# A decoder block in one launch: values copied into both halves of the array, and the embedding's projection moved to the attention

## The chip, the cores and the metric

The kernel runs on one core of a Trainium2 chip. The metric is the device time of one execution in microseconds (us). The engines of the core have a queue each and work through it in order: PE (TensorE: matrix products), DVE (VectorE) and ACT (ScalarE) for elementwise work, POOL (GpSimd, hardly used here) and SP (SyncE, which here only issues DMA transfers). ACT issues some transfers too, in its own order between its other work. Engines wait for each other by semaphores. On-chip memory is SBUF; products land in PSUM, from which DVE and ACT read.

## The reference, cut to what matters

One layer, 256 tokens, width 2048, all in float32. Attention and state-space branch are mixed by gates, then come a feed-forward network and an embedding that is added through a gate.

```python
def hybrid_layer(x, p_i, ...):
    h = rms_norm(x, norm_mix_w)
    q, k, v, z, xbc, dt_raw, gate_a, gate_s = jnp.split(h @ w_in, ...)
    attn = sliding_window_attention(rms(q), rms(k), v, attn_sinks, rel_bias_table) @ w_attn_out
    ssm = mamba2_mixer(z, xbc, dt_raw, ...) @ w_ssm_out
    x = x + (sigmoid(gate_a) * attn + sigmoid(gate_s) * ssm) @ w_out
    u = causal_depthwise_conv(rms_norm(x, norm_ffn_w) @ w_ffn_up, ...)
    g, up = jnp.split(u, 2, axis=-1)
    x = x + (gelu(g) * up) @ w_ffn_down
    ple_gate = sigmoid(rms_norm(x, ple_norm_w) @ w_ple_gate)
    return x + ple_gate * (p_i @ w_ple_proj)      # p_i: (256, 256), w_ple_proj: (256, 2048)
```

The attention has 32 heads of 64, four groups of keys and values (8 heads share one), a window of 128 tokens, a bias by distance and a sink per head. The bias is a table (32 distances' buckets by 32 heads); the kernel gets it by a product with a one-hot matrix.

## The kernel before, in words

**Products.** Every weight matrix is cut into panels of 256 output columns, a panel into chunks of four k-steps of 128 rows (512 KB, or 256 KB for the embedding's two k-steps). A chunk is loaded by SP into a buffer `raw` (five of them), ACT copies it rounded into `wh` (line 71), DVE computes the remainder `wl` (line 72); of `wh` and `wl` there are three each. Activations stand as two rounded parts side by side. A k-step is four products: `wh` against both parts (512 columns, line 87), twice, and `wl` against the first part (256 columns, line 89), twice. The two results of a panel are accumulated in two of the four PSUM banks `acc`; then ACT copies the second part out (`lo`, line 133) and DVE adds (`sum`, line 135). Other products use four more banks, `ms`.

**Stages.** State-space branch with its products (XS: the normalised input); gate panels; `w_ssm_out` over YS; then the attention: the K panel and the V panel (`by_token`, lines 553 to 555), and eight panels for queries in turn with eight gate panels by the list ATT_ORDER; then `w_attn_out` over AS, `w_out`, the feed-forward network, and the tail: eight panels of `w_ple_gate` over XG.

**Attention.** Heads go in 16 pairs. A pair is a Python generator (`attend`), and after each weight chunk `advance` moves up to three running pairs by one step: bias load (by ACT's queue); transpose of the queries (line 610) and their split Q (616, 617); scores (623, 624), bias (626, 627), maxima (629, 630); exponentials on ACT (640) and scaling on DVE (647); transposes of the probabilities (653) and their copies `pts` (654); products with V (662); and the split of the result into AS (140, 141). The products with V have 64 stationary columns: the first head of a pair writes to partitions 0 to 63 and the second to 64 to 127, in three steps of 128 columns. When the list of panels ends, the last pairs are moved to their end (the drain).

**Embedding.** In the tail a function `embedding` computes, one panel ahead of its use, the two k-steps of `p @ w_ple_proj` with the same helpers, into `ms` banks.

**What sets the order.** A scheduler puts every engine's instructions in an order of its own by its model of durations, with the program's order as a priority; then each engine's order is fixed. Buffers of a name share slots, and the memory of a pool that has been released is reused: the attention's small tiles, `tab` among them, take over YS's memory, so they wait for the last product that reads YS.

Of the kernel before, what the change touches and what calls it, by code (L numbers as in the profile page):

```python
# [10 lines left out]
F32 = mybir.dt.float32  # L11
F32R = mybir.dt.float32r
# [33 lines left out]
def hybrid_block(ctx: ExitStack, tc: tile.TileContext, a: dict, out: bass.AP):  # L46
# [10 lines left out]
    def acc():  # L57
        return acc_pool.tile([P, 512], F32, name="acc")

    def misc():  # L60
        return ms_pool.tile([P, 512], F32, name="ms")
# [76 lines left out]
    def split(dst, src):  # L138

        S.activation(dst[:, 0:T], src, AF.Copy)  # L140
        V.tensor_tensor(dst[:, T:2 * T], src, dst[:, 0:T].bitcast(F32), ALU.subtract)
# [347 lines left out]

    m_pool = tc.alloc_tile_pool(name="mp", bufs=1, side="right")  # L490
# [3 lines left out]
    with tc.tile_pool(name="att", bufs=2) as ap:  # L494
# [5 lines left out]
        oneh = ap.tile([N_BUCKETS + 1, RLEN], F32, name="oneh", bufs=1)  # L500
# [3 lines left out]
        rsb = ap.tile([N_HEADS, RLEN], F32, name="rsb", bufs=1)  # L504
# [4 lines left out]
        def pair_bias(i):  # L509
            t = ap.tile([P, 2, 2 * P], F32, name="bias", bufs=4)  # L510
            nc.scalar.dma_start(t, bass.AP(rdr.tensor, rdr.offset + 2 * i * RLEN, [[1, P], [RLEN, 2], [1, 2 * P]]))
            return t
# [80 lines left out]
        vt = ap.tile([P, 2, 256], F32, name="vt", bufs=1)  # L593
        psv = by_token()
        for b in range(2):
            vu = ap.tile([P, 256], F32, name="ksq")
            V.tensor_scalar(vu, psv[b][:, 0:PW], r_tok[:, b:b + 1], None, ALU.mult)
            pv = misc()
            TE.matmul(pv[:, 0:PW], lhsT=flip, rhs=vu, start=True, stop=True)
            S.activation(vt[:, b, :], pv[:, 0:PW], AF.Copy)  # L600

        def attend(i, qn):
# [52 lines left out]
            yield  # L655
            o = misc()
            vs = slice(g * HD, (g + 1) * HD)
            for cs, b, ks, f, e in ((slice(0, P), 0, slice(0, P), True, True),
                                    (slice(P, T), 0, slice(P, T), True, False),
                                    (slice(P, T), 1, slice(T, 384), False, True)):  # L660
                for h in range(2):
                    TE.matmul(o[h * HD:(h + 1) * HD, cs], lhsT=vt[:, b, vs], rhs=pts[:, h, ks], start=f, stop=e)  # L662
            split(AS[:, i, :], o[:, 0:T])
# [11 lines left out]
        for kind, pn in ATT_ORDER:  # L675
            if kind == "q":
                qn = normed(by_token(advance))
                waiting += [(2 * pn, qn), (2 * pn + 1, qn)]
                continue
            ps2 = panel(W, base, ND, XS, between=advance)  # L680
            base += CH
            for i in range(2):
                t = summed(ps2[i])
                V.tensor_tensor(GA[:, 2 * pn + i, :], t, r_bc, ALU.mult)
        while waiting or running:
            advance()
# [77 lines left out]
    with tc.tile_pool(name="ple", bufs=2) as pp:  # L764
        pt_ = pp.tile([P, 2, T], F32, name="pt_", bufs=1)
        nc.scalar.dma_start(pt_, a["pT"])
        PS_ = pp.tile([P, 2, 2 * T], F32R, name="PS_", bufs=1)
        for k in range(2):
            split(PS_[:, k, :], pt_[:, k, :])
        _, r3_bc = stat_to_rstd([sqb], "ple")  # L770
        def embedding(pn):
            wh, wl = load_chunk(a["w_ple_proj"][pn], 2, PW)
            ps2 = [misc(), misc()]
            for k in range(2):
                products(ps2, wh[:, k, :], wl[:, k, :], PS_[:, k, :], k == 0, k == 1)
            return [summed(ps, "ple", 4, pp) for ps in ps2]

        for pn in range(8):
            if pn:
                es = embedding(pn)  # L780
            ps2 = panel(a["w_ple_gate"], pn * CH, ND, XG, joined=(pn == 7))
            if not pn:
                es = embedding(pn)
# [114 lines left out]
```

## Time and profile before

| | |
|---|---|
| Median of three runs | 2064.15 us (2063.41 to 2065.93) |
| The profiled execution | 2064.66 us, its span 2062.9 us |
| PE busy | 2035.7 us, 99% |
| DVE, ACT busy | 1451.1 us (70%), 1171.5 us (57%) |
| Chain that ended last | PE 87%, ACT 2%, DVE 1% |

PE is busy nearly all the time, so the first thing to look for are the few stretches in which it isn't. The times of instructions on PE overlap: an instruction's length is longer than the distance to the next, and what a group of them costs is read from start to start. A fp32 product (not split into rounded parts) shows as two instructions.

### The profile page before, as it was taken

To read this page: it belongs to the slowest core of one execution; us is meant where nothing else is said; L and a number is where in the kernel's file an instruction comes from. 1 tells how busy PE (TensorE), PEld (TensorE's weight loads), DVE (VectorE), ACT (ScalarE), POOL (GpSimd) and SP (SyncE) were. 2 spreads that over 40 slices of the span, in tenths; PEclk is the share of its full clock that TensorE was granted. 3 is DMA by queue.
4 is the path that set the end of the run, shared out by engine and by line. 5 is a ranking of instruction groups with operands and counts; after the bars stand their busy time and mean duration, and the time that the engine had idled before them with its cause. 6 is when DMAs were issued, how large, how long until landed. Compare 5 with 4: busy or idle time off the path is not lost.

```text
span 2062.9 us, 32543 instructions
## 1 busy us (share of the span) xinstructions
PE 2035.7 (99%) x12448; PEld 1797.2 (87%) x12448; DVE 1451.1 (70%) x2502; ACT 1171.5 (57%) x1878; POOL 60.2 (3%) x54
## 2 busy tenths in 40 slices
PE   8999999999999999999989999999999999999999
PEld 7888888888888889998868888888888888888888
DVE  7888787778655546777766677777777776555576
ACT  6686677665544444656555556555555555444454
POOL 0000000000000000100000120000000000000000
PEclk9999999999999999999999999999999999999999
DMA  7556555545555556544435655555555555555564
GB/s 254 206 173 204 183 185 184 194 155 183 189 189 194 189 189 197 179 163 159 165 102 194 234 196 186 193 187 193 194 188 190 194 188 190 194 189 189 186 203 148
DMA packets 113736, 385.50 MB, mean 187 GB/s; under 512 B 13995, under 2 KB 21036, under 8 KB 112428
## 3 DMA queue, kind: packets, MB, share of 16 engines
q1 hardware_dynamic: 104492, 366.00, 51.8%
q10 hardware_dynamic: 9088, 17.43, 2.4%
q8 instruction: 97, 1.59, 0.3%
q14 instruction: 59, 0.48, 0.1%
HBM read 381.16 MB, written 2.21 MB: 186 GB/s over the span
## 4 chain that ended last, share of the span: by engine, by line
PE 87%; ACT 2%; DVE 1%; issue 0%; DVEq 0%
PE acc L87 51%; PE acc L89 26%; PE acc L554 2%; PE acc L553 2%; PE acc L555 2%; PE ms L662 1%; PE ms L653 1%; ACT E L238 1%; PE acc L95 1%; PE ms L451 0%; ACT wh L71 0%; PE ms L87 0%; PE ms L624 0%; PE ms L623 0%; DVE wl L72 0%; ACT L240 0%
## 5 line engine op out<-in xcount | busy, mean ns | idle before, releaser
L72 DVE TENSOR_TENSOR wl<-raw,wh 128x1024 fp32r<-128x1024 f32 (+1 forms) x704 | 846.6, 1205 | 536.3 <-ACT wh L71 533.1
L71 ACT ACTIVATE wh<-raw 128x1024 fp32r<-128x1024 f32 (+1 forms) x704 | 733.3, 1044 | 774.9 <-PE acc L87 459.6
L87 PE MATMUL acc<-XS,wh 128*128 128x512 f32 x1792 | 564.8, 397 | 9.4 <-ACT wh L71 9.4
L87 PE MATMUL acc<-XG,wh 128*128 128x512 f32 x1632 | 506.5, 392 | 0.0
L89 PEld LDWEIGHTS acc<-XS,wl 128*128 128x128 f32 x1792 | 335.1, 189 | 81.3 <-DVE wl L72 8.7
L89 PEld LDWEIGHTS acc<-XG,wl 128*128 128x128 f32 x1632 | 306.4, 188 | 67.4
L89 PE MATMUL acc<-XS,wl 128*128 128x256 f32 x1792 | 361.2, 282 | 3.7 <-DVE wl L72 3.6
L89 PE MATMUL acc<-XG,wl 128*128 128x256 f32 x1632 | 322.3, 279 | 0.0
L87 PEld LDWEIGHTS acc<-XS,wh 128*128 128x128 f32 x1792 | 275.6, 189 | 13.3 <-ACT wh L71 10.2
L87 PEld LDWEIGHTS acc<-XG,wh 128*128 128x128 f32 x1632 | 247.2, 188 | 0.0
L87 PE MATMUL acc<-FS,wh 128*128 128x512 f32 x704 | 218.4, 392 | 0.0
L87 PE MATMUL acc<-YS,wh 128*128 128x512 f32 x512 | 158.8, 392 | 0.0
L89 PEld LDWEIGHTS acc<-FS,wl 128*128 128x128 f32 x704 | 132.2, 188 | 29.0
L89 PE MATMUL acc<-FS,wl 128*128 128x256 f32 x704 | 138.9, 279 | 0.0
L89 PEld LDWEIGHTS acc<-YS,wl 128*128 128x128 f32 x512 | 96.1, 188 | 21.2
L87 PEld LDWEIGHTS acc<-FS,wh 128*128 128x128 f32 x704 | 106.6, 188 | 0.0
L89 PE MATMUL acc<-YS,wl 128*128 128x256 f32 x512 | 101.0, 279 | 0.0
L554 PE MATMUL acc<-wl,XS 128*128 128x256 f32 x320 | 90.9, 284 | 0.0
L555 PE MATMUL acc<-wh,XS 128*128 128x256 f32 x320 | 90.1, 282 | 0.0
L553 PE MATMUL acc<-wh,XS 128*128 128x256 f32 x320 | 90.1, 282 | 0.0
L87 PE MATMUL acc<-AS,wh 128*128 128x512 f32 x256 | 82.9, 401 | 2.9 <-DVE sum L135 1.8
L87 PE MATMUL acc<-MS,wh 128*128 128x512 f32 x256 | 79.4, 392 | 0.0
(233 smaller groups left out, 2106.7 us busy)
## 6 DMA issues: line engine op xcount, KB each, us to landing
raw<-in_w_in SPq DMA_DIRECT2D x256, 512.0 KB, 3.5
raw<-in_w_ffn_up SPq DMA_DIRECT2D x176, 512.0 KB, 3.2
raw<-in_w_ffn_down SPq DMA_DIRECT2D x88, 512.0 KB, 3.2
raw<-in_w_ssm_out SPq DMA_DIRECT2D x64, 512.0 KB, 3.2
raw<-in_w_attn_out SPq DMA_DIRECT2D x32, 512.0 KB, 4.2
raw<-in_w_out SPq DMA_DIRECT2D x32, 512.0 KB, 4.3
raw<-in_w_ple_gate SPq DMA_DIRECT2D x32, 512.0 KB, 3.2
acb<-acd ACTq DMA_DIRECT2D x8, 1024.0 KB, 4.6
```

The costliest lines, as they stand in the source:

```text
L71: S.activation(wh[:, ks, :], raw[:, ks, :], AF.Copy)
L72: V.tensor_tensor(wl[:, ks, :], raw[:, ks, :], wh[:, ks, :].bitcast(F32), ALU.subtract)
L87: TE.matmul(ps, lhsT=wh[:, cs], rhs=x, start=first, stop=False, skip_group_check=True)
L89: TE.matmul(ps[:, 0:T], lhsT=wl[:, cs], rhs=x[:, 0:T], start=False, stop=last, skip_group_check=True)
L95: TE.matmul(ps[:, 0:T], lhsT=w[:, cs], rhs=x[:, h * T:(h + 1) * T], start=first and n == 0, stop=last and n == 2)
L238: S.activation(E[:, h, :], acb[:, h, c, :], AF.Relu, scale=-1.0, bias=acs[:, c, hs.start + h:hs.start + h + 1])
L553: TE.matmul(ps2[b][:, 0:PW], lhsT=hi, rhs=wh[:, k, :], start=(kk == 0), stop=False)
L554: TE.matmul(ps2[b][:, 0:PW], lhsT=hi, rhs=wl[:, k, :], start=False, stop=False)
L555: TE.matmul(ps2[b][:, 0:PW], lhsT=lo, rhs=wh[:, k, :], start=False, stop=(kk == ND - 1))
L653: TE.transpose(pt[:, d * P:(d + 1) * P], Ls[:, h, c:c + P], ident)
L662: TE.matmul(o[h * HD:(h + 1) * HD, cs], lhsT=vt[:, b, vs], rhs=pts[:, h, ks], start=f, stop=e)
```

## The change

Four edits. The values `vt` are stored with each group's 64 columns twice, so that one product yields both heads in both halves of the partitions: two products a pair (512 and 256 columns) in place of six, and the split of the result by halves. The one-hot matrix and the row `rsb` take slots of the `raw` buffers, `bias` has three buffers in place of four. The embedding's eight panels stand behind the last gate panel, before the drain, with an `advance` after each; their accumulators are `acc` banks, and their sums go to a DRAM tile `emb` by SP's queue. The tail loads them from there by ACT's queue.

```diff
+    emb = dram.tile([ND, P, T], F32, name="emb")
...
-        oneh = ap.tile([N_BUCKETS + 1, RLEN], F32, name="oneh", bufs=1)
+        oneh = wp.tile([P, RLEN], F32, name="raw", bufs=5)[0:N_BUCKETS + 1, :]
         nc.sync.dma_start(oneh, a["onehot"])
...
-        rsb = ap.tile([N_HEADS, RLEN], F32, name="rsb", bufs=1)
+        rsb = wp.tile([P, RLEN], F32, name="raw", bufs=5)[0:N_HEADS, :]
...
-            t = ap.tile([P, 2, 2 * P], F32, name="bias", bufs=4)
+            t = ap.tile([P, 2, 2 * P], F32, name="bias", bufs=3)
...
-        vt = ap.tile([P, 2, 256], F32, name="vt", bufs=1)
+        vt = ap.tile([P, 2, N_KV, 2, HD], F32, name="vt", bufs=1)
...
-            S.activation(vt[:, b, :], pv[:, 0:PW], AF.Copy)
+            for h in range(2):
+                S.activation(vt[:, b, :, h, :], pv[:, 0:PW].rearrange("p (g d) -> p g d", g=N_KV), AF.Copy)
...
             o = misc()
-            vs = slice(g * HD, (g + 1) * HD)
-            for cs, b, ks, f, e in ((slice(0, P), 0, slice(0, P), True, True),
-                                    (slice(P, T), 0, slice(P, T), True, False),
-                                    (slice(P, T), 1, slice(T, 384), False, True)):
-                for h in range(2):
-                    TE.matmul(o[h * HD:(h + 1) * HD, cs], lhsT=vt[:, b, vs], rhs=pts[:, h, ks], start=f, stop=e)
-            split(AS[:, i, :], o[:, 0:T])
+            ov = o.rearrange("p (h t) -> p h t", h=2)
+            vd = vt.rearrange("p b g h d -> p b g (h d)")
+            TE.matmul(ov, lhsT=vd[:, 0, g, :], rhs=pts[:, :, 0:T], start=True, stop=False, skip_group_check=True)
+            TE.matmul(ov[:, :, P:T], lhsT=vd[:, 1, g, :], rhs=pts[:, :, T:384], start=False, stop=True,
+                      skip_group_check=True)
+            for h in range(2):
+                split(AS[half[h], i, :], ov[half[h], h, :])
...
+        pt_ = wp.tile([P, 2, T], F32, name="raw", bufs=5)
+        nc.sync.dma_start(pt_, a["pT"])
+        PS_ = ap.tile([P, 2, 2 * T], F32R, name="PS_", bufs=1)
+        for k in range(2):
+            split(PS_[:, k, :], pt_[:, k, :])
+        for pn in range(8):
+            wh, wl = load_chunk(a["w_ple_proj"][pn], 2, PW)
+            ps2 = [acc(), acc()]
+            for k in range(2):
+                products(ps2, wh[:, k, :], wl[:, k, :], PS_[:, k, :], k == 0, k == 1)
+            for i in range(2):
+                nc.sync.dma_start(emb[2 * pn + i], summed(ps2[i]))
+            advance()
         while waiting or running:
             advance()
...
-            if pn:
-                es = embedding(pn)
+            es = []
+            for i in range(2):
+                t = pp.tile([P, T], F32, name="ple", bufs=4)
+                nc.scalar.dma_start(t, emb[2 * pn + i])
+                es.append(t)
             ps2 = panel(a["w_ple_gate"], pn * CH, ND, XG, joined=(pn == 7))
-            if not pn:
-                es = embedding(pn)
```

The edits also move instructions that they don't name. First SP, from the last weights of `w_ssm_out` to the K panel's weights (`raw<-in_w_in`); before:

```order
29 L70 DMA raw<-in_w_ssm_out 128x1024 x64
30 L70 DMA raw<-in_w_in 128x1024 x7
31 L499 DMA tab<-in_rel_bias_table 32x32
32 L501 DMA oneh<-in_onehot 33x384
33 L515 DMA sink<-in_sinks 128x32
34 L519 DMA gq<-in_qk_gain 128x2
35 L564 DMA flip<-in_flip 128x128
36 L70 DMA raw<-in_w_in 128x1024 x65
```

and now:

```order
29 L70 DMA raw<-in_w_ssm_out 128x1024 x64
30 L502 DMA raw<-in_onehot 33x384
31 L500 DMA tab<-in_rel_bias_table 32x32
32 L516 DMA sink<-in_sinks 128x32
33 L520 DMA gq<-in_qk_gain 128x2
34 L565 DMA flip<-in_flip 128x128
35 L70 DMA raw<-in_w_in 128x1024 x72
```

Seven weight loads that stood ahead of `tab` stand behind it and the three small loads. On PE the product of `tab` and the one-hot matrix, which stood after 41 products of the K panel, is now the first behind YS.

Second, PE at the end of the drain (653 and 655: transposes of the probabilities; 662 and 663: products with V; AS: attention output), before:

```order
3592 L653 MATMUL ms<-c_ident,Ls 128x128 x6
3593 L662 MATMUL ms<-pts,vt 64x128 x6
3594 L653 MATMUL ms<-c_ident,Ls 128x128 x6
3595 L87 MATMUL acc<-AS,wh 128x512 x2
3596 L89 MATMUL acc<-AS,wl 128x256 x2
3597 L87 MATMUL acc<-AS,wh 128x512 x2
3598 L89 MATMUL acc<-AS,wl 128x256 x2
3599 L662 MATMUL ms<-pts,vt 64x128 x6
```

and now:

```order
3670 L655 MATMUL ms<-c_ident,Ls 128x128 x6
3671 L662 MATMUL ms<-pts,vt 128x512
3672 L663 MATMUL ms<-pts,vt 128x2x128
3673 L655 MATMUL ms<-c_ident,Ls 128x128 x6
3674 L662 MATMUL ms<-pts,vt 128x512
3675 L663 MATMUL ms<-pts,vt 128x2x128
3676 L87 MATMUL acc<-AS,wh 128x512 x2
3677 L89 MATMUL acc<-AS,wl 128x256 x2
```

Two k-steps of the attention output moved behind the last product with V. The embedding's products (PS_) stand earlier; their last ones, and the next transposes of a pair (it is pair 12, counted from 0), now:

```order
3562 L87 MATMUL acc<-PS__10959,wh 128x512
3563 L89 MATMUL acc<-PS__10959,wl 128x256
3564 L87 MATMUL acc<-AS,wh 128x512
3565 L89 MATMUL acc<-AS,wl 128x256
3566 L87 MATMUL acc<-AS,wh 128x512
3567 L89 MATMUL acc<-AS,wl 128x256
3568 L87 MATMUL acc<-AS,wh 128x512
3569 L89 MATMUL acc<-AS,wl 128x256
3570 L87 MATMUL acc<-AS,wh 128x512
3571 L89 MATMUL acc<-AS,wl 128x256
3572 L87 MATMUL acc<-AS,wh 128x512
3573 L655 MATMUL ms<-c_ident,Ls 128x128 x6
```

All 64 of them stand between the last product of the gates (row 3491) and this place.

## Rows read from the trace of the kernel before

**Rows 1.** the page: span; busy time and share of each engine.
```profile
span 2062.9 us, 32543 instructions
...
PE 2035.7 (99%) x12448; PEld 1797.2 (87%) x12448; DVE 1451.1 (70%) x2502; ACT 1171.5 (57%) x1878; POOL 60.2 (3%) x54
```

**Rows 2.** windows (length, busy times (instructions), granted clock, DMA share, GB/s).
```profile
1024.80:1045.80 21.00, 21.00 (x135) 18.36 (x133) 13.33 (x27) 16.45 (x34) 0.00 (x0) 1.00 0.50 164
1045.80:1071.30 25.50, 16.38 (x101) 12.60 (x99) 14.38 (x45) 13.18 (x40) 0.00 (x0) 0.87 0.09 31
...
1058.00:1065.00 7.00, 5.78 (x27) 4.75 (x28) 2.91 (x14) 4.19 (x14) 0.00 (x0) 0.52 0.00 1
```

**Rows 3.** PE timeline, drain (start, length, work; in brackets the wait).
```profile
1058.67 1.54 PE L653 MATMUL ms<-c_ident,Ls 128*128 128x128 f32 x6 [2.37 <-DVE Ls L647]
```

**Rows 4.** PE timeline of the tail, one embedding panel.
```profile
1995.41 0.62 PE L87 MATMUL ms<-PS__19888,wh 128*128 128x512 f32 x2
...
1996.79 0.39 PE L87 MATMUL acc<-XG,wh 128*128 128x512 f32 x1
```

**Rows 5.** PE timeline, products with V in one run.
```profile
1036.77 0.28 PE L89 MATMUL acc<-AS,wl 128*128 128x256 f32 x1
1036.98 0.88 PE L662 MATMUL ms<-pts,vt 128*64 128x128 f32 x12
...
1038.00 0.28 PE L624 MATMUL ms<-kl,Q 128*128 128x256 f32 x1
```

**Rows 6.** chain by time, products with V in two runs.
```profile
1018.33 0.36 PE ms L662 x2
...
1019.24 0.80 PE ms L662 x10
```

**Rows 7.** PE timeline, full fp32 products of 128 columns.
```profile
93.11 0.28 PE L89 MATMUL acc<-XS,wl 128*128 128x256 f32 x1
93.23 1.06 PE L443 MATMUL ms<-cbm,xde 128*128 128x128 f32 x8
...
94.25 0.63 PE L87 MATMUL acc<-XS,wh 128*128 128x512 f32 x2
```

**Rows 8.** SP timeline where the K panel begins.
```profile
775.23 5.85 SPq L70 DMA_DIRECT2D raw<-in_w_in  x3
781.44 0.34 SPq L499 DMA_DIRECT2D tab<-in_rel_bias_table  x1
...
783.15 0.43 SPq L564 DMA_DIRECT2D flip<-in_flip  x1
783.68 11.50 SPq L70 DMA_DIRECT2D raw<-in_w_in  x4
```

**Rows 9.** DMA issues (KB each, median us to landing).
```profile
raw<-in_w_in SPq DMA_DIRECT2D x256, 512.0 KB, 3.5
...
gno<-in_ssm_norm SPq DMA_DIRECT2D x1, 16.0 KB, 1.7
tab<-in_rel_bias_table SPq DMA_DIRECT2D x1, 4.0 KB, 4.0
```

**Rows 10.** PE and clock after an idle stretch early in the kernel.
```profile
215.35 1.22 PE L87 MATMUL acc<-XS,wh 128*128 128x512 f32 x2 [2.99 <-ACT wh L71]
...
215.30:222.00 6.70, 6.61 (x19) 5.12 (x20) 5.14 (x8) 4.44 (x7) 0.00 (x0) 0.50 0.68 234
```

**Rows 11.** ACT groups by shape (count, busy us, mean ns).
```profile
L133 ACT ACTIVATE lo<-acc 128x256 f32<-128x256 f32 x142 | 45.7, 372 | 2.5 <-PE acc L89 2.4
...
L640 ACT ACTIVATE Ls<-Ls,nm 128x256 f32<-128x256 f32 x32 | 16.0, 501 | 2.8 <-DVE nm L632 2.8
...
L71 ACT ACTIVATE wh<-raw 128x512 fp32r<-128x512 f32 x24 | 14.4, 622 | 8.1 <-issue 6.2 <-DMA raw<-in_w_in 0.9 <-PE acc L87 0.9
...
L694 ACT ACTIVATE GA<-GA 128x2048 f32<-128x2048 f32 x2 | 3.8, 1917 | 0.0
...
L694 ACT ACT_TABLE_LOAD x2 | 2.6, 1283 | 0.0
```

More of the change, by code (lines that the diff above doesn't have):

```diff
@@ L764, in hybrid_block @@
     with tc.tile_pool(name="ple", bufs=2) as pp:
[L765 to L769, printed above, removed]
-        _, r3_bc = stat_to_rstd([sqb], "ple")
[L771 to L776, printed above, removed]
-        for pn in range(8):
-            if pn:
-                es = embedding(pn)
+        _, r3_bc = stat_to_rstd([sqb], "ple")
+        for pn in range(8):
+            es = []
[3 more added lines that the diff above has]
+                es.append(t)
             ps2 = panel(a["w_ple_gate"], pn * CH, ND, XG, joined=(pn == 7))
-            if not pn:
-                es = embedding(pn)
             for i in range(2):
```

## The prediction

> **What bounds the kernel now.** I read the page's busy times first: PE is busy 2035.7 of 2062.9 us [rows 1], so an edit pays only where it takes products off PE or closes one of PE's few gaps, and it costs wherever it opens a new one. Next came the windows around the attention. Up to 1045.8 PE is full; from 1045.8 to 1071.3 it works 16.38 of 25.5 us, so 9.1 us are empty, and from 1058 to 1065 the granted clock is 0.52 [rows 2]. This is the drain: the last pairs of heads are softmax chains through DVE and ACT, and PE waits for them, up to 2.37 us at once [rows 3]. Then the timeline of the tail, for what the embedding's products cost where they stand. Then the timeline of the place where the K panel begins (781 us), because the order of SP changes there. The profiled execution took 2064.66 us, 0.5 over the median of the runs; the sum is made against it.
>
> **The embedding's products leave the tail.** A panel of them lies there between 1995.41 and 1996.79, among products that leave PE no gap [rows 4]: 1.38 us, eight panels, 11.0 us taken off a full PE. This gain is sure, and what the change does is decided by what the same 11.0 us cost in the new place. If they all filled empty time, the whole 9.1 us of the drain and some of its half clock would be won.
>
> **Where they stand now.** By the order of the changed program all 64 embedding products stand on PE before the transposes of pair 12, directly behind the last gate panel. There, between 1024.8 and 1045.8, PE was full before [rows 2]. The drain itself (the last two pairs: transposes, products with V, transposes, products with V) has no embedding product in it, and the two k-steps of the attention output that stood between its last two steps now stand behind them. So the embedding pushes later work back by its own length and the drain keeps its waits. Net of leaving the tail: 11.0 - 11.0 = 0.
>
> **What it meets there.** A chunk of the embedding is 1.38 us for PE; ACT has for it one conversion of 0.622 and two evacuations of 0.372 [rows 11], 1.37 us. So ACT has as much to do for it as PE, and has other work queued between. From the first embedding conversion to the evacuation of chunk 6's first half, ACT's order holds 8 conversions (5.0), 15 evacuations (5.6), one full weight conversion (at twice 0.622, 1.2), the sigmoid of the gates (1.92), two table loads (2.6), eight exponentials (at 0.501, 4.0) and eight copies for pairs 10 to 12 (at 0.372, 3.0): 23.3 us. The three weight buffers let ACT begin at most eight k-steps of 0.69 us (half a panel of the embedding [rows 4]) and some 2.5 us of attention products, 8.0 us, ahead of PE; I allow 3 us in which ACT itself waits for PE. It is done 23.3 - 8.0 + 3 = 18.3 us after PE begins the embedding, DVE's sum as much later as an evacuation takes. PE needs that accumulator (there are four) for the first product of the attention output after 11.0 us of embedding, 1.3 of V products, 1.0 of scores and perhaps 1.5 of smaller waits: 14.8. The wait is 3.9 us, with the smaller ones 5.4. Bounds: 0 if ACT's own waits vanish and it begins early, 9 if pair 12's exponentials come late too. I take 5.4. In the drain I credit 1.5 us: the two k-steps behind the last V products cover the waits for the last pair's result and for an accumulator. Against that each pair's output is now copied by halves, two ACT and two DVE instructions in place of one each, which lengthens its chain by about 0.4. Between -4 and +2, I take -1.5.
>
> **The K panel's first weights.** The one-hot matrix now takes a slot of the weight buffers, and with that the scheduler has drawn SP's order differently. Before, seven weight loads stood ahead of the load of the bias table, tab; now tab, sink, gains and flip stand ahead of all of them. tab's memory is freed by the last product with YS: its load was issued at 781.44, when those products ended, with the K panel's first loads already on their way since 775.23 [rows 8]. SP is in order, so all K panel loads now wait for the end of the YS products, and PE has nothing else: its next instruction is the small product with tab, then the K panel. The steps: tab at 781.44, three small loads, the first weight load some 0.45 earlier than the 783.68 of before (one load fewer between), 783.2; landing 3.5 later [rows 9], 786.7. On ACT the store of rdr stands ahead of the conversion and waits for the small product, so for tab: issue 781.44 plus 1.7 (the fastest small load) to 4.0 [rows 9], plus product, copy and issue, some 2 us, gives 785.1 to 787.4, about the same. Conversion of hi (at twice 0.622, 1.2) and of the remainder (as long): PE runs fully from 789.1. It lost 789.1 - 781.2 = 7.9, less some 0.9 of the small product that is now inside the stall (two instructions of 384 columns at 0.114 per 128 columns [rows 7], and 0.2 of entry): 7.0. Between 5.5 and 8.5 by the two ends of the landings. The nearest row for the clock is 215.35: after 2.99 us without work the granted clock is 0.50 through 6.7 us [rows 10], in which full work loses 3.3. So between 0 (it falls and is back before the work is) and 3.4 more; I take 2.5, nearer to the row. Nothing later gives this back, since PE is the bound. Together 9.5. bias with three buffers in place of four is no cost: its reloads stand behind the reads they wait for.
>
> **V in both halves.** Before, six products of 64 columns a pair; two halves run at once, and run and changes of mode hold PE from 1036.77 to 1038.00 [rows 5], 1.23 less the two normal steps of 0.115 around it, 1.0 us. Ten of the sixteen pairs are split in two runs by the order, and a split one holds PE for 0.36 + 0.80 [rows 6] and pays entry and exit, 0.2, twice: 1.56. 6 x 1.0 + 10 x 1.56 = 21.6 us. Now two full products over 512 and 256 columns. A full fp32 product of 128 columns takes two instructions, and eight of them hold PE from 93.11 to 94.25 less two steps of 0.115, 0.91, so 0.114 each [rows 7]; 768 columns are 12 of these, 1.37, or less, since fewer instructions carry it. At 1.33, 16 x 1.33 = 21.3, so -0.3. Between -1 and +4 (if entering fp32 costs 0.2 again).
>
> The Trainium skill (TensorEngine Tiling (Array Packing), Theoretical Speedup) speaks against this edit: with 64 stationary columns two tiles work at once, up to twice as fast, and the full form gives that up. The same page (Key Properties) says that a change of mode drains TensorE, and the trace agrees: 1.0 us held for some 0.65 of products. By the first rule alone the kernel would come to about 2088 (the fourth rival); with the drains counted, V is even.
>
> **Sum.** 0 (embedding) + 5.4 (waits beside it) - 1.5 (drain) + 9.5 (K panel) - 0.3 (V) = +13.1. From 2064.66 that is 2077.8; beside the median, 2077.
>
> **Rivals.** First, the drain is filled: ACT and DVE bring pairs 13 to 15 forward under the embedding, so that little is left to wait for. It wins up to 9.1, and with the half clock of 1058 to 1065 (5.78 busy, half of it lost, 2.9) [rows 2] 12.0; with the K panel's 9.5 and V's -0.3, -2.8, and -5 with the K panel at its lower end: 2062 to 2060. For it: the order was drawn to run other work beside the pairs. Against it: the last two pairs stand as bare as before. It decides from the point where the drain loses more than 9 us; 0.09. Second, it is filled by half and the embedding meets no waits: 9.5 - 0.3 - 7 = +2, 2066, no change; 0.09. Third, a load queue: SP now holds 16 stores of the embedding between the loads of the attention output, each waiting for a sum; if ACT's delay reaches them, one or two weight loads come late by a landing of 3.5 us: 2077.8 + 5 = 2083; 0.15. For it: SP is in order; against it: five weight slots ahead. Fourth, the changes of mode were hidden and the old form cost only its six pairs of instructions, 6 x 0.114 = 0.68 a pair: then V loses 16 x 0.65 = 10.4, 2088; against it stands the 1.0 us held [rows 5]; 0.04. The forecast has 0.63.
>
> **How the numbers follow.** A measurement can tell 0.2%, 4.1 us. Slower: forecast 0.63, third 0.15, fourth 0.04, and a third of the second 0.03: 0.85. Same: the rest of the second and a quarter of the first: 0.08. Faster: 0.07. The likeliest case alone spans 2070 to 2084 (K panel 5.5 to 11.9, embedding 0 to 9, not all at one end). The range reaches to the second rival: 2065 to 2085, which leaves out most of the first and the fourth.
>
> **What would show it.** Right: a wait of PE of some 7 us at 781, ended by the hi conversion, with half clock behind it; SP's first K load behind tab; PE gaps between the last gate panel and pair 12's transposes, released by sums and evacuations; the drain's bare steps as before; a tail shorter by 11 us. Wrong: PE full at 781, or a drain with less than 4 us empty.

## The result and the profile after

The changed kernel takes 2078.93 us (median of four runs, 2077.99 to 2080.30) against 2064.54 of the kernel before in the same comparison: ratio 1.0068, 95% interval 1.0056 to 1.0080. It is slower. The profiled execution took 2078.69 us, its span is 14.0 us longer than that of before.

The page of the changed kernel, span and busy times, answers to [rows 1]:

```profile
span 2076.9 us, 32419 instructions
...
PE 2037.7 (98%) x12320; PEld 1796.9 (87%) x12320; DVE 1460.1 (70%) x2518; ACT 1179.1 (57%) x1896; POOL 61.8 (3%) x54
```

PE's busy time grew by 2.0 us only, so twelve of the fourteen are empty time. To find it I cut the span at three products on PE that every kernel here has: the last that reads YS (w_ssm_out ends), the last that reads AS (attention output ends) and the last that reads FS (feed-forward ends). In us:

| | to YS's end | YS's end to AS's last | AS's last to FS's last | FS's last to the end |
|---|---|---|---|---|
| before | 781.09 | 358.04 | 817.92 | 105.82 |
| after | 780.54 | 384.11 | 817.93 | 94.32 |

The third column repeats to 0.01 us. So the stretches can be compared one by one, and the attention's stretch, with 11.0 us of embedding in it, is 26.1 us longer while the tail is 11.5 shorter. The waits of PE in it come in three places. First the K panel; the queue of SP there, from the changed kernel's timeline, answers to [rows 8]:

```profile
780.89 0.32 SPq L500 DMA_DIRECT2D tab<-in_rel_bias_table  x1
781.26 0.41 SPq L516 DMA_DIRECT2D sink<-in_sinks  x1
781.73 0.42 SPq L520 DMA_DIRECT2D gq<-in_qk_gain  x1
782.20 0.43 SPq L565 DMA_DIRECT2D flip<-in_flip  x1
782.72 1.80 SPq L70 DMA_DIRECT2D raw<-in_w_in  x4
```

On ACT, the store of rdr and the conversion behind it (start, length; in brackets the wait):

```profile
785.29 0.33 ACTq L508 DMA_DIRECT2D rdr<-raw  x1
786.37 1.06 ACT L71 ACTIVATE wh<-raw 128x1024 fp32r<-128x1024 f32 x1 [4.98 <-DMA raw<-in_w_in]
```

And PE's waits from there to the end of the drain, from its timeline (the embedding's products are those that read PS_; the drain answers to [rows 3]):

```profile
782.45 0.90 PE L504 MATMUL ms<-raw,tab 33*32 33x384 f32 x2 [1.64 <-DVE T L486]
787.48 0.80 PE L554 MATMUL acc<-wh,XS 128*128 128x256 f32 x2 [4.13 <-ACT wh L71]
788.74 0.58 PE L555 MATMUL acc<-wl,XS 128*128 128x256 f32 x1 [0.46 <-DVE wl L72]
...
1045.87 0.79 PE L87 MATMUL acc<-PS__10959,wh 128*128 128x512 f32 x1 [2.08 <-DVE sum L135]
...
1074.95 0.39 PE L625 MATMUL ms<-kh,Q 128*128 128x256 f32 x1 [1.15 <-DVE Q L619]
...
1083.94 1.54 PE L655 MATMUL ms<-c_ident,Ls 128*128 128x128 f32 x6 [2.50 <-DVE Ls L649]
1086.21 2.08 PE L662 MATMUL ms<-pts,vt 128*128 128x512 f32 x2 [0.73 <-ACT pts L656]
...
1091.34 1.12 PE L662 MATMUL ms<-pts,vt 128*128 128x512 f32 x2 [0.95 <-ACT pts L656]
...
1094.69 0.74 PE L87 MATMUL acc<-AS,wh 128*128 128x512 f32 x2 [0.39 <-DVE AS L141]
...
1098.30 0.51 PE L87 MATMUL acc<-AS,wh 128*128 128x512 f32 x1 [1.92 <-DVE sum L135]
```

The windows of the three places (length, busy times of PE, PEld, DVE, ACT, POOL, granted clock, DMA share, GB/s) answer to [rows 2]:

```profile
780.54:790.54 10.00, 3.77 (x15) 2.51 (x14) 4.65 (x10) 2.77 (x4) 0.00 (x0) 0.62 0.65 221
790.54:800.00 9.46, 9.46 (x74) 9.46 (x73) 3.67 (x3) 4.07 (x4) 0.00 (x0) 0.86 0.79 264
1028.94:1049.61 20.67, 16.54 (x79) 12.87 (x78) 16.57 (x43) 18.30 (x42) 0.00 (x0) 0.92 0.72 231
1049.61:1098.30 48.69, 38.66 (x201) 30.66 (x199) 29.10 (x70) 24.84 (x62) 0.00 (x0) 0.89 0.33 108
```

The K panel's stall is 6.2 us of empty PE, and the granted clock stays low well after it. Beside the embedding 4.1 us are empty, and ACT is busy for 18.30 of 20.67 us. From there to the end of the drain 10.0 are empty, where before it was 9.1. The waits for `pts` right ahead of the products with V are new or longer.

### The profile page after: what moved, and what is told of

It reads as the page before. It is cut to its first block, busy times and chain, and to the rows that moved or that the text cites. A ratio compares the mean times of both kernels' runs of the same rounds, so it can differ in the third digit from the quotient of the medians.

```text
span 2076.9 us, 32419 instructions
## 1 busy us (share of the span) xinstructions
PE 2037.7 (98%) x12320; PEld 1796.9 (87%) x12320; DVE 1460.1 (70%) x2518; ACT 1179.1 (57%) x1896; POOL 61.8 (3%) x54
## 4 chain that ended last, share of the span: by engine, by line
PE 86%; ACT 2%; DVE 1%; DMA 0%; issue 0%; SPq 0%; DVEq 0%; ACTq 0%
PE acc L87 50%; PE acc L89 26%; PE acc L555 2%; PE acc L556 2%; PE acc L554 2%; PE ms L662 1%; ACT E L238 1%; ACT wh L71 1%; PE acc L95 1%; PE ms L451 0%; PE ms L655 0%; DVE wl L72 0%; PE ms L663 0%; PE ms L626 0%; PE ms L625 0%
```

## The experiments

Each kernel ran beside the kernel before on its chip. For them the table gives the same stretches as above, the empty time of PE between the gates' last product and the last AS product, the median, and the ratio to the kernel before with its interval. FS's last to the end is 105.82 or 105.83 where the embedding stands in the tail, 94.31 to 94.33 where it stands in the attention (fill_early: 94.52).

| | to YS's end | YS's end to AS's last | empty | AS's last to FS's last | median | ratio |
|---|---|---|---|---|---|---|
| before | 781.09 | 358.04 | 9.1 | 817.92 | | |
| after | 780.54 | 384.11 | 14.2 | 817.93 | 2078.93 | 1.0068 (1.0056 to 1.0080) |
| raw_only | 783.51 | 367.76 | 9.0 | 817.93 | 2074.62 | 1.0046 (1.0032 to 1.0060) |
| small_early | 781.24 | 381.70 | 13.9 | 817.92 | 2076.95 | 1.0055 (1.0042 to 1.0067) |
| v_old | 784.28 | 381.68 | 12.7 | 817.92 | 2079.32 | 1.0067 (1.0054 to 1.0079) |
| no_embedding_move | 781.62 | 367.27 | 12.4 | 817.92 | 2074.43 | 1.0046 (1.0034 to 1.0059) |
| bias_before_YS | 789.50 | 374.40 | 14.5 | 817.93 | 2077.92 | 1.0065 (1.0052 to 1.0077) |
| V_alone | 786.11 | 360.76 | 11.7 | 817.93 | 2073.42 | 1.0045 (1.0031 to 1.0059) |
| fill | 790.14 | 371.77 | 12.7 | 817.92 | 2075.93 | 1.0046 (1.0033 to 1.0059) |
| fill_v_old | 791.13 | 367.34 | 8.4 | 817.92 | 2071.02 | 1.0032 (1.0019 to 1.0045) |
| bias_at_start | 787.57 | 377.75 | 15.6 | 819.64 | 2081.05 | 1.0075 (1.0062 to 1.0087) |
| six_sums | 780.82 | 384.93 | 14.3 | 817.93 | 2080.15 | 1.0070 (1.0057 to 1.0084) |
| fill_best | 788.65 | 364.35 | 7.1 | 819.59 | 2069.60 | 1.0021 (1.0013 to 1.0030) |
| fill_early | 779.27 | 365.59 | 6.9 | 819.80 | 2060.87 | 0.9981 (0.9972 to 0.9990) |

The first column needs care: before, after, raw_only, v_old and six_sums run the same work up to YS's end, and it ends between 780.54 and 784.28. A comparison of whole executions carries some of that spread of 3.7 us; a stretch from YS's end on does not. One source of the spread stands in the last section.

**raw_only**, one part of the change alone:

```diff
-        oneh = ap.tile([N_BUCKETS + 1, RLEN], F32, name="oneh", bufs=1)
+        oneh = wp.tile([P, RLEN], F32, name="raw", bufs=5)[0:N_BUCKETS + 1, :]
...
-        rsb = ap.tile([N_HEADS, RLEN], F32, name="rsb", bufs=1)
+        rsb = wp.tile([P, RLEN], F32, name="raw", bufs=5)[0:N_HEADS, :]
```

> The kernel before with one edit of the change alone: the one-hot matrix and rsb take slots of the weight buffers (V, bias and the embedding as before). SP's order has tab, sink, gains and flip ahead of all K panel loads, as in the changed kernel. Theory (the load of tab waits for the last YS product and holds the K panel's weights behind it): PE waits 6 us at 781, with half clock behind it for some 3 us of loss, and the kernel takes 2064.5 + 9 = 2073.5 us (2071 to 2076). Rival (the stall of the changed kernel has another source, its V or its embedding): no wait at 781, 2064.5 us (2063 to 2066).

Measured 2074.62, and the attention's stretch is 9.72 us longer than before. PE's long wait at the K panel:

```profile
790.60 0.80 PE L553 MATMUL acc<-wh,XS 128*128 128x256 f32 x2 [4.36 <-ACT wh L71]
```

The stall is the changed kernel's, with neither its V nor its embedding. What this doesn't tell is whether the order of SP or the two lent slots make it.

**small_early**, from the changed kernel: the four small loads out of YS's memory.

```diff
+        small = ev.tile([P, T], F32, name="rsq", bufs=2)
-        tab = ap.tile([N_BUCKETS + 1, N_HEADS], F32, name="tab", bufs=1)
+        tab = small[0:N_BUCKETS + 1, 0:N_HEADS]
...
-        sink = ap.tile([P, N_HEADS], F32, name="sink", bufs=1)
+        sink = small[:, N_HEADS:2 * N_HEADS]
...
-        flip = ap.tile([P, P], F32, name="flip", bufs=1)
+        flip = small[:, P:T]
```

> The changed kernel with tab, sink, gains and flip in one tile of the buffer rsq, whose memory is not YS's; SP issues the four loads early in the kernel, so that nothing that waits for YS stands ahead of the K panel's weights. The one-hot matrix and rsb still take two of the five weight slots. Theory (SP's order is the cause): PE is full at 781 (under 1 us empty, granted clock 1.00), 9 us less than the changed kernel, 2070 us (2068 to 2072). Rival (the two slots taken from the weight buffers are the cause, the order is not): the first K loads still come after 778, PE waits 4 us or more at 781 to 792, and the kernel stays at 2075 to 2079 us.

Measured 2076.95: the theory's number fails, and so does the rival's mechanism, because the K panel's loads now start at 769.86. SP, then ACT, then PE:

```profile
764.34 0.36 SPq L503 DMA_DIRECT2D raw<-in_onehot  x1
769.86 29.76 SPq L70 DMA_DIRECT2D raw<-in_w_in  x11
```

```profile
783.09 0.33 ACTq L509 DMA_DIRECT2D rdr<-raw  x1
783.52 2.95 ACT L71 ACTIVATE wh<-raw 128x1024 fp32r<-128x1024 f32 x3 [1.43 <-DVE T L486]
```

```profile
784.63 0.50 PE L555 MATMUL acc<-wh,XS 128*128 128x256 f32 x2 [2.35 <-ACT wh L71]
785.89 0.58 PE L556 MATMUL acc<-wl,XS 128*128 128x256 f32 x1 [0.76 <-DVE wl L72]
```

The weights are there, and ACT, in order, first waits for the copy of the small product (behind DVE's T) to store rdr. Half of the empty time goes (6.2 to 3.1 us), and the clock falls all the same: 0.50 from 786 to 790, 0.76 from 790 to 794. A second queue had stood behind the first.

**v_old**, from the changed kernel:

```diff
-            TE.matmul(ov, lhsT=vd[:, 0, g, :], rhs=pts[:, :, 0:T], start=True, stop=False, skip_group_check=True)
...
+            for cs, b, ks, f, e in ((slice(0, P), 0, slice(0, P), True, True),
+                                    (slice(P, T), 0, slice(P, T), True, False),
+                                    (slice(P, T), 1, slice(T, 384), False, True)):
+                for h in range(2):
+                    TE.matmul(o[h * HD:(h + 1) * HD, cs], lhsT=vt[:, b, g, 0, :], rhs=pts[:, h, ks], start=f, stop=e)
+            split(AS[:, i, :], o[:, 0:T])
```

> The changed kernel with the old six products with V a pair, of 64 columns, and the split of the result in one piece (vt is still stored twice; its first copy is read). Theory (the two forms take PE equally long, 21.6 against 21.3 us in all): 2079 us, within 1.5. Rival A (the full products cost more, since two halves ran at once): 2069 us. Rival B (the split by halves lengthens the drain): 2 to 4 us less than the changed kernel, and shorter waits of PE between 1066 and 1095.

Measured 2079.32, by the median as the theory has it. But this execution reached YS's end 3.7 us later than the changed kernel's, and from there on it is 2.4 us shorter: rival B's number. I took the stretch for it.

**no_embedding_move**, from small_early: the embedding back in the tail, in `ms` banks, without `emb`.

> The kernel before with V in both halves, the one-hot matrix and rsb in weight slots, bias with three buffers, and the four small loads early as in small_early: all of the change but the embedding's move, and without the late K panel. Theory (V is even, and a late K panel and the embedding carry the whole loss): 2064.5 us, the time of the kernel before, within 2. Rival (V in both halves costs by its form or by the drain): 2068 to 2075 us. Against small_early it prices the embedding's move alone: by the theory 5.5 us.

Measured 2074.43, against the theory. Its attention stretch is 9.2 us longer than before with no embedding in it: the K panel's rest (6.5, this run less V_alone below) and V. Against small_early the embedding costs 381.70 - 367.27 - 11.51 = 2.9 us, where 5.5 was expected.

**bias_before_YS**, from small_early: the lines from `tab` to the store of `rdr`, with `sink`, `gq` and `flip`, stand ahead of the loop of w_ssm_out.

> The changed kernel with the bias table's whole preparation (tab, one-hot, their product, rsb, the store of rdr) and the loads of sink, gains and flip moved ahead of w_ssm_out, out of YS's memory; one-hot and rsb still take weight slots. Theory after small_early (two queues held the K panel's weights back, first SP by the load of tab, then ACT by the store of rdr, which stands ahead of the conversions and waits for the small product): no wait of PE over 0.5 us between the last YS product and 800, clock 1.00 there, and 9.7 us less than the changed kernel (the price of the edit in raw_only from the end of YS on): 2069 us (2067 to 2071). Rival (the two weight slots hold up something of their own, now at the start of w_ssm_out): a wait of 2 us or more there, 2071 to 2075 us.

Measured 2077.92, above both ranges. The K panel is as the theory has it: no wait there, clock 1.00, and from YS's end on exactly 9.71 us less than the changed kernel. But the wait came back at the new place, as the rival had it, PE and then the window behind it (0.77 in the next four us):

```profile
609.87 1.22 PE L87 MATMUL acc<-YS,wh 128*128 128x512 f32 x2 [2.91 <-ACT wh L71]
```

```profile
610.00:614.00 4.00, 3.96 (x11) 2.85 (x12) 3.35 (x3) 1.72 (x2) 0.00 (x0) 0.50 0.41 144
```

On ACT the store of rdr and the last panel's evacuations stand ahead of the conversions there too (607.78, the conversions from 608.78). The chain product, copy, store on ACT's queue doesn't cost by itself: the kernel before has it at the K panel without a wait of PE, with its own memory for the one-hot matrix and `rsb` and with conversions at 781.16 and 784.23 ahead of the store at 788.45. Both places with a wait have lent weight slots and, with them, an order of ACT that puts the store first. No run lends the slots without the chain, so more than that isn't shown.

**V_alone**, from bias_before_YS: the embedding back in the tail.

> The kernel before with V in both halves (two products a pair, split by halves) and the bias preparation ahead of w_ssm_out as in bias_before_YS; the embedding stays in the tail. Theory after v_old and no_embedding_move (V's edit costs 2.4 us, by longer waits in the drain, since the pairs' steps fall otherwise, not by its products): PE empty for 12 us between the gates' end and the last AS product, against 9.1 before, and 2067 us (2065 to 2069). Rival (V is even, as predicted; what no_embedding_move lost was the late K panel alone): 2064.5 us, within 1.

Measured 2073.42, above the theory's range, with the wait at YS's start in it. From YS's end on it is 2.72 us longer than before, and 11.7 us are empty against 9.1: the theory's size. The busy rest is 360.76 - 11.67 = 349.1 us against 348.9 before, so the products themselves are even. Part of the empty time is here, PE's timeline:

```profile
1038.20 0.73 PE L87 MATMUL acc<-AS,wh 128*128 128x512 f32 x2 [1.58 <-ACT wh L71]
...
1067.07 2.08 PE L660 MATMUL ms<-pts,vt 128*128 128x512 f32 x2 [1.01 <-ACT pts L654]
1072.20 2.08 PE L660 MATMUL ms<-pts,vt 128*128 128x512 f32 x2 [0.92 <-ACT pts L654]
```

At 1067.07 and 1072.20 transposes, copy to `pts` and product with V of one pair follow each other with nothing between; before, two k-steps of the attention output stood between the last steps. The wait at 1038.20 is another thing: a weight conversion stands on ACT behind a table load and four exponentials. Neither the kernel before nor the changed one has a wait there, so 1.6 of the 2.7 us come from this kernel's own order.

**fill**, from bias_before_YS: the attention output's first panel of products is issued ahead of the embedding, both behind the drain's loop.

```diff
         while waiting or running:
             advance()
+        early = [panel(a["w_attn_out"], 0, ND, AS)]
+        for pn in range(8):
+            embed(pn)
```

> bias_before_YS with the embedding's eight panels put, in the program, behind the first panel of the attention output, whose products now stand behind the drain's last advance: by the order of the engines 40 of the 64 embedding products then lie between the steps of the last four pairs, the others just ahead of them, and 56 products of the attention output lie among the last pair's steps. Theory (the drain stayed empty only because the embedding stood ahead of it): the empty time of PE between the gates' end and the last AS product falls from 14.2 to under 6 us, the half clock there goes too, 2069 - 8 - 2 = 2059 us (2056 to 2063), faster than the kernel before. Rival (ACT and DVE are the bound there: their conversions, evacuations and sums push the pairs' own chains back by as much): 2066 to 2071 us, with waits on DVE's Ls and sum still over 1.5 us.

Measured 2075.93, the theory's number missed by far (the wait at YS's start is in it again, 610.60). From YS's end on it is 2.6 us less than bias_before_YS, 12.7 us are empty, and the rival's marks are there, waits for Ls and for sums:

```profile
1045.58 0.91 PE L654 MATMUL ms<-c_ident,Ls 128*128 128x128 f32 x6 [3.49 <-DVE Ls L648]
...
1072.00 0.50 PE L87 MATMUL acc<-PS__10956,wh 128*128 128x512 f32 x1 [2.34 <-DVE sum L135]
```

**fill_v_old**: fill with v_old's edit.

> fill with the old six products with V a pair and the split in one piece. Theory (the form of V costs nothing by itself; where the drain is filled, what it adds to a pair's chain is hidden): the time of fill, within 2 us. Rival A (the full products cost time): 2 to 10 us less than fill. Rival B (the changes of mode of the split products cost more once they lie between more other products): 2 us or more above fill.

Measured 2071.02. From YS's end on it is 4.43 us less than fill. Rival A has the number and not the mechanism: 4.32 of the 4.43 are empty time (12.67 to 8.35), the busy rest is the same to 0.1 us. With the six products the scheduler places the pairs' steps otherwise. Against bias_before_YS, filling and the old form together win 7.1 us.

**bias_at_start**, from the changed kernel: the bias preparation ahead of the very first panels, its loads on ACT's queue, tab, one-hot and rsb in weight slots; sink and gains among the constants; flip loaded behind the K panel.

> The changed kernel with the bias preparation (tab, one-hot, their product, rsb, the store of rdr) at the very start of the kernel, sink and gains among the constants, and flip loaded behind the K panel's loads. No weight slot is lent out at the start of YS or of the K panel, and neither SP nor ACT has a waiting transfer ahead of the K panel's weights: eight conversions stand between the evacuations there, as in the kernel before. Theory (small_early and bias_before_YS moved the wait from SP to ACT's queue and from one stage's start to another; only the removal of both ends it): PE full from 775 to 800 and from 600 to 615, and the whole 9.7 us of raw_only come back: 2069 us (2067.5 to 2071). Rival (the changed kernel's loss lies mostly in the embedding and the drain, and what was seen at 781 is given back by waits later on): 2073 us or more.

Measured 2081.05, 12 us above the theory's number. PE is full at 600 and from 770 to 800, so both waits can be ended. They were paid at the start instead, PE's timeline:

```profile
6.18 1.46 PE L199 MATMUL ms<-raw 33*32 33x384 f32 x2 [6.18 <-DMA raw<-in_onehot]
12.55 1.22 PE L87 MATMUL acc<-XS,wh 128*128 128x512 f32 x2 [4.92 <-ACT wh L71]
```

YS ends 7 us later than in the changed kernel. The attention's stretch is 6.4 shorter, not 9.7; the same order of products there took 3.4 us longer than in bias_before_YS, 1.1 of it empty and most of the rest in the clock (0.94 from 1020 to 1050).

**six_sums**, from the changed kernel, where DVE's sum ahead of the 2.08 us wait shows this line:

```profile
1045.39 0.86 DVE L135 TENSOR_TENSOR sum<-acc,lo 128x256 f32<-128x256 f32 x2 [2.02 <-DMA emb<-sum]
```

```diff
-                nc.sync.dma_start(emb[2 * pn + i], summed(ps2[i]))
+                nc.sync.dma_start(emb[2 * pn + i],
+                                  summed(ps2[i], *(("rsq", 2) if (2 * pn + i) % 3 == 2 else ())))
```

> The changed kernel with every third sum of the embedding in a buffer of rsq (two, idle there) in place of sum, so that six sums can stand in place of four. In the changed kernel the longest wait beside the embedding (2.08 us at 1045.87) ends by a sum that waited 2.02 us for a store of emb to leave its buffer. Theory (the stores, 4.6 us from issue to landing, hold the four sum buffers): no wait of DVE's sum for a DMA, the wait of 2.08 falls under 0.7, the half clock behind it goes, and the kernel takes 2 to 4 us less than the changed one, 2075.5 us. Rival (ACT's work is what is late, as the prediction had it): the wait stays above 1.2 us with ACT's lo as its cause, 2078 to 2080 us.

Measured 2080.15, the attention's stretch 0.8 us longer than the changed kernel's. The theory falls. No sum waits for a transfer any more, DVE and then PE:

```profile
1048.96 0.42 DVE L135 TENSOR_TENSOR sum<-acc,lo 128x256 f32<-128x256 f32 x1 [2.09 <-ACT lo L133]
```

```profile
1046.92 0.49 PE L87 MATMUL acc<-PS__10959,wh 128*128 128x512 f32 x1 [0.57 <-DVE rsq L135]
1049.44 0.50 PE L87 MATMUL acc<-AS,wh 128*128 128x512 f32 x1 [1.55 <-DVE sum L135]
```

The sum now waits 2.09 us for ACT's `lo`, which stands behind a table load and four exponentials. 2.08 us in one place became 0.57 + 1.55 = 2.12 in two. ACT is late there, the stores were only as late as ACT.

**fill_best**: fill_v_old with bias_at_start's preparation.

> fill_v_old with the bias preparation at the start as in bias_at_start: the embedding's panels between the last pairs' steps, six products with V a pair, no late K panel. Theory (fill_v_old lost only the wait at the start of YS against the kernel before; from the end of YS to the last AS product it took 9.3 us more than the kernel before and 11.0 of embedding leave the tail, with 0.5 lost there): 1.3 to 2.3 us less than the kernel before, 2062.5 us (2060 to 2064.5). Rival (the fill of the drain depends on the shift in time, and its waits come back): 2066 us or more.

Measured 2069.60, the rival's number, but not by its mechanism: the waits of the drain don't come back (7.1 us are empty). The start cost 7.6 us against the kernel before, as in bias_at_start; from YS's end on it took 1278.25 us against 1281.78, 3.5 less. 1.7 us of a larger gain went in the stage that reads MS, which no row had announced.

**fill_early**, from fill_best: the preparation in the second group of the state-space branch, its store on POOL's queue.

```diff
+            if g == 1:
+                rdr = dram.tile([N_HEADS, RLEN], F32, name="rdr")
+                tab = ev.tile([P, T], F32, name="lo", bufs=4)[0:N_BUCKETS + 1, 0:N_HEADS]
...
+                for cs in (slice(0, T), slice(T, RLEN)):
...
+                    TE.matmul(ps[0:N_HEADS, cs], lhsT=tab, rhs=oneh, start=True, stop=True)
+                    rsb = ev.tile([P, T], F32, name="sum", bufs=4)[0:N_HEADS, 0:n]
+                    V.tensor_copy(rsb, ps[0:N_HEADS, cs])
+                    nc.gpsimd.dma_start(rdr[:, cs], rsb)
...
-    MS = ms_pool2.tile([P, ND * 2 * T + 488], F32R, name="MS")[:, 0:ND * 2 * T].rearrange("p (k t) -> p k t", k=ND)
+    MS = ms_pool2.tile([P, ND * 2 * T + 454], F32R, name="MS")[:, 0:ND * 2 * T].rearrange("p (k t) -> p k t", k=ND)
```

> fill_best with two differences. The bias preparation stands in the second group of the state-space branch, in buffers lo and sum, its store on POOL's queue, so that the start of the kernel is as in the kernel before. And the padding of MS is 454 in place of 488, which moves MS by the 136 bytes by which sink and gains among the constants moved the weight buffers. Theory: the 7.6 us that fill_best lost before the end of YS against the kernel before are gone; from there on it took 3.5 us less than the kernel before; and its 1.7 us in the stage that reads MS (89.9 against 88.2 us) come from the distance between MS and the weights and go too: 2059.5 us (2057.5 to 2062), faster than both kernels, MS stage 88.2. Rival A (the stage of MS was slower for another reason): 89.9 there again, 2061 us. Rival B (the preparation opens a wait wherever it stands among panels): a wait of over 2 us between 220 and 290 or at 781, 2063 us or more.

Measured 2060.87 against 2064.42 of the kernel before, ratio 0.9981 (0.9972 to 0.9990): a small gain over the kernel before. Of it 1.9 us stand from YS's end on (1279.91 against 1281.78), the rest ahead of it and within the spread. Its windows (780 to 800; beside the pairs; the drain):

```profile
780.00:800.00 20.00, 20.00 (x180) 19.87 (x180) 12.49 (x19) 7.93 (x11) 1.64 (x1) 1.00 0.69 228
1020.00:1045.00 25.00, 21.57 (x130) 17.70 (x129) 17.31 (x48) 18.77 (x45) 0.00 (x0) 0.95 0.41 126
1045.00:1080.00 35.00, 31.55 (x185) 24.87 (x185) 23.73 (x58) 21.10 (x52) 0.00 (x0) 0.94 0.55 175
```

The K panel is full at full clock, and 6.9 us are empty between the gates and the last AS product, with the embedding's 11.0 us of products among them, against 9.1 before without. Rival A has the MS stage: it stays slow, the padding changed nothing.

## Why the prediction was right, and where it wasn't

2077.0 was predicted, 2078.9 measured, inside the range; slower was given 0.85. The runs take the loss apart, from the end of YS on, each part as the difference of two kernels. They are chosen so that they add up:

| part | predicted | measured | from |
|---|---|---|---|
| K panel | +9.5 | +9.7 | raw_only less before; after less bias_before_YS |
| V and drain | -0.3 - 1.5 = -1.8 | +2.7 | V_alone less before |
| embedding | 0 + 5.4 = +5.4 | +2.1 | (bias_before_YS less V_alone) 13.64, less the tail's 11.50 |
| up to YS's end | 0 | -0.55 | after less before, within the spread |
| sum | +13.1 | +14.0 | |

So the total is better than its terms: on this split two errors, +4.5 and -3.3, nearly cancel, and that is luck. How the second and the third row divide depends on the kernels subtracted: V_alone's wait at 1038.20, which the changed kernel doesn't have, is a loss in the one and a gain in the other. Read in the changed kernel's own windows, the drain has 10.0 us empty against 9.1, so +0.9, and 4.1 are empty beside the embedding. By either reading the forecast was too low for the drain and too high for the embedding.

**The K panel** is right in place, cause and size. SP's first K load stood behind tab at 782.72 (783.2 predicted), the conversion ended PE's wait, and PE ran fully from 788.74 (789.1). The loss divides otherwise than I had it: 6.2 us empty, where I had 7.0, and some 3.3 of clock (raw_only's 9.72 less its 6.47 empty), where I had taken 2.5 out of 0 to 3.4. The prediction held SP's order alone for the cause and saw the store of rdr as no later than the weights. small_early shows that it was a second cause of its own, hidden behind the first: with SP repaired, 6.5 to 7.3 of the 9.7 us stay (no_embedding_move less V_alone; small_early less bias_before_YS). Behind both orders stand the lent slots: raw_only lends them and changes nothing else, and it has the whole 9.7; fill_early lends none to the bias table, and its K panel has no wait.

**V in both halves** is even in its products, as predicted: 349.1 against 348.9 us busy in V_alone, 0.1 apart between fill and fill_v_old. The fourth rival falls: had the old form cost only its instructions, ten us would stand there. By the Trainium skill (TensorEngine Tiling (Array Packing), Theoretical Speedup) two tiles at once may be up to twice as fast; these runs have no such gain. The same page's remark under Key Properties that a change of mode drains TensorE fits that; no run separates the drains from the rest.

**The drain** is the step that failed. I credited 1.5 us because "the two k-steps behind the last V products cover the waits for the last pair's result and for an accumulator". Before, PE and one row of ACT:

```profile
1060.76 1.92 PE L662 MATMUL ms<-pts,vt 128*64 128x128 f32 x12 [0.55 <-ACT pts L654]
...
1065.95 0.88 PE L662 MATMUL ms<-pts,vt 128*64 128x128 f32 x12
1067.78 0.74 PE L87 MATMUL acc<-AS,wh 128*128 128x512 f32 x2 [0.94 <-DVE AS L141]
...
1071.26 0.50 PE L87 MATMUL acc<-AS,wh 128*128 128x512 f32 x1 [1.82 <-DVE sum L135]
```

```profile
1060.21 0.87 ACT L654 ACTIVATE pts<-ms 128x384 f32<-128x384 f32 x2
```

and ACT in the changed kernel, whose rows of PE stand above:

```profile
1085.29 0.87 ACT L656 ACTIVATE pts<-ms 128x384 f32<-128x384 f32 x2
...
1090.40 0.38 ACT L140 ACTIVATE AS<-ms 64x256 fp32r<-64x256 f32 x1
1090.80 0.49 ACT L656 ACTIVATE pts<-ms 128x384 f32<-128x384 f32 x1
```

The two k-steps covered part of the wait for the result (0.94 before, 0.39 now) and nothing of the wait for an accumulator (1.82 and 1.92), which follows the last product of their own panel. And they had stood between the last pair's transposes and its products with V, which began at 1065.95 without a wait; now 0.95 opens there. A filler that moves was counted as a gain and not as a move. The new form of V adds to it in two ways, of which the forecast had the second alone, as 0.4 more. Its first product reads both heads and so follows both copies to `pts` (they end at 1086.16, it starts at 1086.21); before, the first products began while the second copy still ran. And the copy of the result by halves stands between the last pair's two copies to `pts` (1090.40). Together the waits for `pts` are 2.1 us where before 0.55 stood, and a wait for Q of 1.15 is new; a wait for Ls of 1.10 (1047.04 before) is gone. The term measured +0.9 in place of -1.5, within its bounds of -4 to +2 but on the other side of zero.

**Beside the embedding** the mechanism is right in the main: PE waits for sums, and ACT is late. The waits of after there are 4.0 us (0.49, 0.56, 0.88, 2.08), with half clock behind the last. The place is another: 2.08 comes at the seventh panel of the embedding, and the first AS product (1049.61), where the forecast had 3.9, waits for nothing. And the longest wait ended by a store that held a sum's buffer, which the forecast didn't have. six_sums shows by failing that ACT stood behind it: with the hold gone, the same time is lost to `lo`, 1.55 us of it at the first AS product. The net price of 2.1 comes mostly from 4.4 us of waits in bias_before_YS, against which stand V_alone's 1.58 at 1038.20 and the tail, which gave 11.5 in place of 11.0.

**The rivals.** The filled drain didn't come in the changed kernel, as the order said. But the gain exists in another order: fill, which mixes the embedding with the pairs, wins 2.6 us with the new form of V, and fill_v_old 7.1 with the old one (which alone is worth 2.4 in v_old). That fill wins no more I put down to ACT and DVE, for which its waits stand; no run separates that from the order. By its own terms this rival's -5 should have been -6.8 (5.5 - 0.3 - 12.0). The load queue (third rival) isn't in the trace: PE waits for no weights in the changed kernel's attention output.

## What to carry to other kernels

A tile moved to other memory moves loads: look at each in-order queue for what now stands ahead of the weights, and when one is repaired, look at the next queue before expecting the time back. Work put beside a latency chain pays where the engines' orders mix the two and the engines that serve the chain have room: here the embedding brought ACT as much work as PE, and stood ahead of the chain; mixed into it, in fill_early, the same work left 6.9 us empty in place of 9.1. And sum the drain as a list of waits with the filler of each: a filler that moves closes one wait and opens another.

## What the hardware showed that I had not expected

The price of a stall in clock didn't follow its length: 6.5 us empty at the K panel lost 3.3 us to the granted clock behind them (raw_only), and 3.1 us empty lost 2.7 to 3.4 (no_embedding_move less V_alone is 6.51, of which 3.11 are empty there and 0.68 later). Nor was it the same for one length. The wait of 3.0 us at some 215 us is in every kernel here but fill_early. Before, the granted clock is 0.50 through 6.7 us behind it [rows 10]; in the changed kernel, where it ends at 216.08, the clock is back sooner:

```profile
216.00:219.00 3.00, 2.62 (x8) 1.77 (x8) 2.94 (x4) 3.00 (x5) 0.00 (x0) 0.57 0.35 119
219.00:222.00 3.00, 3.00 (x16) 2.64 (x16) 2.20 (x6) 1.47 (x3) 0.00 (x0) 0.86 0.89 305
```

That is one source of the spread up to YS's end.

In the three kernels with sink and gains among the constants and `flip` behind the K panel (bias_at_start, fill_best, fill_early) the stage that reads MS is slower, at a granted clock of 1.00 and with PE never empty. The MS products of 80 us, before and in fill_early:

```profile
1145.00:1225.00 80.00, 80.00 (x465) 70.47 (x464) 0.47 (x2) 0.40 (x1) 1.00 0.59 205
```

```profile
1150.00:1230.00 80.00, 80.00 (x454) 69.33 (x454) 0.84 (x2) 0.40 (x1) 1.00 0.59 202
```

454 products in place of 465: 2%, 1.7 to 1.9 us for the stage. Other stages kept their pace. Moving MS by the constants' 136 bytes didn't change it, and its cause stays open.
